# Four edits to a four-layer hybrid decoder trunk: selection in steps, table copies moved, memory loads held, one rotary product for two groups

## The chip, the cores and the metric

The kernel runs on one core of a Trainium2 chip. The metric is the time of one execution on the device in microseconds; lower is better. One profiled execution gives the trace. Engines: TensorE (PE, with its weight loads as PEld), VectorE (DVE), ScalarE (ACT), GpSimd (POOL) and SyncE (SP). SP issues most DMAs from its own queue, POOL the rest.

## The reference, cut to what matters

A sequence of 256 tokens of width 2048 passes four layers. Each layer normalises, makes one wide input projection, runs one self mixer and a cross-attention over a memory of 256 tokens, gates both with SiLU, projects out and adds to the residual. The mixers are, in order, latent attention (0), sparse attention with key selection (1), window attention with sinks (2) and latent attention again (0).

```python
mem_n = _rmsnorm(mem, mem_norm)
for i in range(DEPTH):
    h = _rmsnorm(x, norm_in[i])
    kind, j = i % N_MIXERS, i // N_MIXERS
    # self_out, mq, gate from the mixer of this kind
    mem_out = _memory_attention(mq, mem_n @ w_mem_kv[i])
    y = jnp.concatenate([self_out, mem_out], axis=-1) * jax.nn.silu(gate)
    x = x + y @ w_out[i]
return _rmsnorm(x, final_norm)
```

In latent attention, queries come from a compressed vector: `q = (_rmsnorm(c_q) @ w_uq)`, 16 heads of 128 plain and 64 rotary features; the rotary part is rotated, and so is one rotary key shared by all heads. In sparse attention a small indexer scores every key for every query (16 index heads, ReLU, weighted sum), the 64 best keys of each query are kept, and a position bias from a table of 32 buckets x 32 heads is added to the logits. Window attention adds the same bias inside a window of 128.

## The kernel before, in words

All products are float32, done as three products of float32r parts: a high part (`copy_act` on ACT, L60) and a low part (`tensor_sub` on DVE, L64). Every weight block is split that way after its load, into `wh` and `wl` (three buffers each, `parts_of`). `stage` (L190) loads one block of weights on the SP queue into `wr`, five buffers of up to 512 KB. `rows_by` (L212) gives outputs with tokens on partitions: for each 128 rows of weights, six matmuls, 2 token halves x 3 parts, as wide as the columns asked for (up to 512). `columns_by` (L232) gives outputs with features on partitions: for each 128 rows, two wide matmuls (512) and two narrow ones (256). Both accumulate in PSUM tiles with the tag "acc", four buffers.

The kernel is written as one straight program. A scheduler with a time simulation reorders the instructions of each engine when the program is built, in general in the order they were written in, as operands and buffers become ready. What goes through `tc.keep_in_program_order` stays behind whatever was written before it on its engine. Tiles with one tag share a few buffers: "pq" has five, "aux" three ("PQ, AUX, WR" at L28).

**Memory stage** (`memory`, L305). For each layer and each half of the heads: a value product (`acc_mv`), two key products (`acc_mk`), whose results POOL stores to DRAM (`mv`, `mkT`). In the first step two bias tables are computed (`bias_table`, L116); one for sparse attention, one for window attention. `table_copies` (L130) then writes each table, a quarter at a time, to DRAM once for each of 128 partitions, so that a later load (`bm`, L775) can read it shifted by one element per partition. In the memory stage one such copy follows each step, two follow the second (L384).

**Layers** (L821). `mixer.first()` makes keys and values. For latent attention it makes the compressed key/value rows and the rotary key with two 288-column products (`acc_kva`, `acc_kvb`), and then the compressed queries (`acc_cq`). Then six parts follow in the order memory 0, self 0 to 3, memory 1. Each part has a projection, an attention, and an output product of its quarter (`w_out`, L827: four column blocks `c`), written one part later. The memory part (`memory_project`, L476) loads its stored keys and values on POOL (`mkr`, tag "pq"; `mvr`, tag "aux"), makes its queries (`acc_mq`) and its gate (`acc_g`, two halves of one `columns_by` each).

A latent self part (`Latent.project`, L605) handles a group of four heads: the rotary query product (`acc_qr`, 4 heads x 64 = 256 columns, 12 row blocks), its rotation (`rope`, L528), split and transposes to `qrT`; then plain queries `acc_qn`, keys `acc_kn`, values `acc_va`, and the gate.

A sparse or window layer (`Grouped`, L664) has `first`, which in the sparse layer calls `select` (L719). `select` makes the index queries (`acc_iq`) and then, for two halves of the queries, 16 score steps (two matmuls `isp`, a ReLU on ACT, a weighted sum on DVE) and 8 steps that each find and strike out the 8 largest scores (`max`, `match_replace`). Behind it `first` clears and fills the spaced values `vz` with POOL, ACT and DVE.

Of the kernel before, what the change touches and what calls it, by code (L numbers as in the profile page):

```python
# [15 lines left out]
P = 128  # L16
S = 256
# [9 lines left out]
N_TAB = 384  # L27
PQ, AUX, WR = 5, 3, 5  # L28


@with_exitstack
def kernel(ctx: ExitStack, tc: tile.TileContext, a: dict, out: bass.AP,
# [97 lines left out]
    def table_copies(v, g):  # L130
        src = bass.AP(tensor=flat[v].tensor, offset=flat[v].offset + g * 8 * N_TAB,
                      ap=[[0, P], [1, 8 * N_TAB]])
        tc.keep_in_program_order(nc.gpsimd.dma_start(tabs[v][g].rearrange("p h n -> p (h n)"), src))


    def rsqrt_mean(dst, ssq, n):
# [53 lines left out]
    def stage(w, k0, m, cols):  # L190
# [13 lines left out]
        return wr, n  # L204

    def parts_of(wr, c0, n):
        wh = wp.tile([P, 512], F32R, name="wh", tag="wh", bufs=3)
        wl = wp.tile([P, 512], F32R, name="wl", tag="wl", bufs=3)
        split(wh[:, :n], wl[:, :n], wr[:, c0:c0 + n])
        return wh, wl  # L210

    def rows_by(xt, kts, w, k0, cols, name, prepare=None):  # L212


        acc = [ps.tile([P, 512], F32, name=f"acc_{name}{t}", tag="acc", bufs=4) for t in range(2)]
        for s in range(0, kts, ST):
            m = min(ST, kts - s)
            wr, n = stage(w, k0 + s, m, cols)
            if prepare is not None and s % 4 == 0:
                prepare(s // 4)  # L220
            for k in range(m):
                wh, wl = parts_of(wr, k * n, n)
                q = xt[(s + k) // 4]
                for t in range(2):
                    xh, xl = (q[:, v, (s + k) % 4, t * P:(t + 1) * P] for v in range(2))
                    first, last = s + k == 0, s + k == kts - 1
                    nc.tensor.matmul(acc[t][:, :n], xh, wh[:, :n], start=first, stop=False)  # L227
                    nc.tensor.matmul(acc[t][:, :n], xh, wl[:, :n], start=False, stop=False)  # L228
                    nc.tensor.matmul(acc[t][:, :n], xl, wh[:, :n], start=False, stop=last)  # L229
        return acc  # L230

    def columns_by(xt, kts, w, k0, cols, name):  # L232

        acc = [ps.tile([P, 2, S], F32, name=f"acc_{name}{j}", tag="acc", bufs=4) for j in range(2)]
        for s in range(0, kts, 2 * ST):
            m = min(2 * ST, kts - s)
            wr, n = stage(w, k0 + s, m, cols)
            for k2 in range(0, m, 2):
                wh, wl = parts_of(wr, k2 * S, 2 * S)
                for k in range(2):  # L240
                    kt = s + k2 + k
                    q = xt[kt // 4]

                    for j in range(2):
                        o = k * S + j * P
                        nc.tensor.matmul(acc[j], wh[:, o:o + P], q[:, :, kt % 4, :],  # L246
                                         start=kt == 0, stop=False)
                    for j in range(2):
                        o = k * S + j * P
                        nc.tensor.matmul(acc[j][:, 0, :], wl[:, o:o + P], q[:, 0, kt % 4, :],  # L250
                                         start=False, stop=kt == kts - 1)
        return acc
# [52 lines left out]
    def memory():  # L305
# [49 lines left out]

        copies = [(v, g) for v in range(2) for g in range(4)]
        for i in range(depth):
            w = a["w_mem_kv"][i]
            for p_ in range(2):
# [22 lines left out]
                if step == 6:  # L382
                    nm.finish()
                for c in copies[:2 if step == 1 else 1]:  # L384
                    table_copies(*c)
                copies = copies[2 if step == 1 else 1:]

# [87 lines left out]

    def memory_project(nm, i, w, mq0, g0, part):  # L476
        kT, qT = [], []
        v = [act.tile([P, 2, 512], F32R, name="mvr", tag="aux", bufs=AUX) for z in range(2)]
        for z in range(2):
            nc.gpsimd.dma_start(v[z], mv[i][part][:, z])  # L480
        for h in range(2):
            k = act.tile([P, 2, 2, S], F32R, name="mkr", tag="pq", bufs=PQ)
            nc.gpsimd.dma_start(k, mkT[i][2 * part + h])
            kT.append(k)
# [54 lines left out]
    class Latent:  # L539
# [6 lines left out]
        def first(self):  # L546
# [55 lines left out]
            for z, sg in zip(self.scale, (1.0, -1.0)):  # L602
                nc.vector.tensor_scalar(z, qr, sg * (A_NOPE + A_ROPE) ** -0.5, None, op0=OP.mult)

        def project(self, g):  # L605

            j = self.j
            wq, wkv = a["w_uq"][j], a["w_ukv"][j]
            qn, kn = [], []
            qr = act.tile([P, 4, S], F32R, name="qrT", tag="aux", bufs=AUX)  # L610
            v = act.tile([P, 2, 512], F32, name="va", tag="aux", bufs=AUX)
            acc = rows_by(self.cT[:3], 12, wq, 0, (g * 768, 4, 192, A_NOPE, A_ROPE), "qr")
            for t in range(2):
                rr = wk.tile([P, 4, A_ROPE], F32, name="qrr", tag="z", bufs=3)
                rope(rr, acc[t][:, :S].rearrange("p (h d) -> p h d", h=4), t, 4)
                rs = wk.tile([P, 4, 2, A_ROPE], F32R, name="qrs", tag="qrs", bufs=1)
                split(rs[:, :, 0, :], rs[:, :, 1, :], rr)
                transposed(lambda i0, i1: qr[:, i0:i1, t * P:(t + 1) * P],
                           [rs[:, h].rearrange("p a b -> p (a b)") for h in range(4)])
            for half in range(2):  # L620
# [10 lines left out]
            for t in range(2):  # L631
                copy_act(v[:, t, :], acc[t])
            return qn, qr, kn, v, gate(self.nm, self.w, self.g0 + g * 512)

# [29 lines left out]
    class Grouped:  # L664
# [7 lines left out]
        def first(self):  # L672
# [10 lines left out]
            if self.sparse:  # L683
                self.select()

# [33 lines left out]
        def select(self):  # L719
# [5 lines left out]
            for n in (8, 4, 4):  # L725
# [10 lines left out]
                h0 += n  # L736
            nc.vector.tensor_scalar(iw, iw, 0.25, None, op0=OP.mult)
            for b in range(2):
                n = (b + 1) * P
                sco = [wk.tile([P, S], F32, name=f"sco{z}", tag=f"sco{z}", bufs=1) for z in range(2)]  # L740
                cur = 0
                for h in range(16):
# [9 lines left out]
                    else:  # L752
                        nc.vector.scalar_tensor_tensor(sco[1 - cur][:, :n], rl[:, :n], c,
                                                       sco[cur][:, :n], op0=OP.mult, op1=OP.add)
                        cur = 1 - cur
                nc.vector.tensor_add(sco[1 - cur][:, :n], sco[cur][:, :n], caus[:, S - n:])
                cur = 1 - cur
                for it in range(8):
                    m8 = small("m8", 8)
                    nc.vector.max(m8, sco[cur][:, :n])  # L760
                    nc.vector.match_replace(sco[1 - cur][:, :n], m8, sco[cur][:, :n], TAKEN)
                    cur = 1 - cur
                nc.vector.tensor_scalar(self.sel[:, b, :n], sco[cur][:, :n], -2e38, NEG,
                                        op0=OP.is_gt, op1=OP.mult)

        def project(self, g):
# [11 lines left out]

        def attend(self, g, q, bm, gT):
            y = act.tile([P, 2, 4, S], F32R, name="y", tag="y", bufs=2)  # L780
            for h in range(8):
# [35 lines left out]

    nm = Norm(0)
    memory()

    for i in range(depth):  # L821
# [5 lines left out]
        def w_out(part, y, last):  # L827
            for c in range(4):
                acc = rows_by([y], 4, a["w_out"][i], part * 4, (c * 512, 512), "wo")
                for t in range(2):  # L830
                    xs = x[t][:, c * 512:(c + 1) * 512]
                    nc.vector.tensor_add(xs, xs, acc[t])  # L832
                if last and nxt is not None:
                    nxt.chunk(c)
# [10 lines left out]
        for n_, part in enumerate(order):  # L845
            if part >= 4:
                y = memory_attend(*memory_project(nm, i, mixer.w, mixer.mq0, mixer.g0, part - 4))
            else:
# [90 lines left out]
```

## Time and profile before

| | |
|---|---|
| time, median of 3 runs | 2635.22 us (2634.94 to 2639.01) |
| time of the profiled execution | 2636.8 us |
| its span in the profile | 2634.7 us |
| TensorE busy | 2601.2 us, 99% of the span |
| VectorE, ScalarE busy | 1884.1 us (72%), 1628.8 us (62%) |
| GpSimd busy | 57.3 us (2%) |
| moved by DMA | 511.70 MB, 194 GB/s in the mean |
| DMA in the first six of 40 slices | 256 to 305 GB/s, busy share 0.8 to over 0.9 |

TensorE's busy time is that of pipelined instructions, so 99% says that it hardly waits, and not that each matmul runs at its best; what one costs is read from the distance between starts. The memory stage fills the first 370 us or so; the four layers follow.

### The profile page before, as it was taken

How to read it: one execution, taken by the hardware profiler on the slowest of the kernel's cores; microseconds unless marked ns; L12 is line 12 of the kernel's file. 1: busy time of each engine (PE TensorE's matmuls, PEld its weight loads, DVE VectorE, ACT ScalarE, POOL GpSimd, SP SyncE). 2: the span in 40 equal slices, each digit the busy share in tenths (PEclk: the TensorE clock that was granted, in tenths of full speed). 3: DMA queues.
4: the chain of work that ended last, by engine and by line, in shares of the span. 5: the costliest groups of instructions: out<-in, count | busy, mean ns of one | idle time of the engine just before them, and what ended most of it. 6: DMA issues, size and time to landing. Idle time of an engine off the chain costs nothing.

```text
span 2634.7 us, 42943 instructions
## 1 busy us (share of the span) xinstructions
PE 2601.2 (99%) x14556; PEld 2254.7 (86%) x14556; DVE 1884.1 (72%) x4171; ACT 1628.8 (62%) x3476; POOL 57.3 (2%) x101
## 2 busy tenths in 40 slices
PE   8999999999999999999999999999999999999998
PEld 7888888888888889888888888888888888888886
DVE  6566656677767685877777776777778767776767
ACT  6455556556656566666666666676666655665655
POOL 1000000000000000000000000000000000000000
PEclk9999999999999999999999999999999999999999
DMA  9889886666557665555555555555555666655764
GB/s 305 279 287 300 281 256 198 166 185 168 169 160 224 192 192 172 167 183 170 173 163 191 188 190 177 173 172 178 189 168 162 205 165 186 165 170 156 226 183 135
DMA packets 456924, 511.70 MB, mean 194 GB/s; under 512 B 69584, under 2 KB 352480, under 8 KB 455552
## 3 DMA queue, kind: packets, MB, share of 16 engines
q1 hardware_dynamic: 443328, 451.75, 56.5%
q0 software_dynamic: 13088, 56.16, 6.6%
q8 instruction: 114, 1.87, 0.3%
q14 instruction: 106, 0.87, 0.1%
q10 hardware_dynamic: 288, 1.05, 0.1%
HBM read 489.91 MB, written 31.56 MB: 198 GB/s over the span
## 4 chain that ended last, share of the span: by engine, by line
PE 97%; DMA 1%; DVE 1%; ACT 0%; issue 0%; SPq 0%; ACTq 0%
PE acc_g L246 14%; PE acc_g L250 7%; PE acc_wo L227 7%; PE acc_wo L228 7%; PE acc_wo L229 7%; PE acc_mq L246 5%; PE acc_mk L246 5%; PE acc_qn L246 3%; PE acc_cq L246 3%; PE acc_mq L250 2%; PE acc_mk L250 2%; PE acc_q L227 2%; PE acc_q L228 2%; PE acc_q L229 2%; PE acc_mv L227 2%; PE acc_mv L228 2%
## 5 line engine op out<-in xcount | busy, mean ns | idle before, releaser
L64 DVE TENSOR_TENSOR wl<-wr,wh 128x512 fp32r<-128x512 f32 (+2 forms) x1776 | 1173.8, 664 | 645.1 <-ACT wh L60 614.2
L60 ACT ACTIVATE wh<-wr 128x512 fp32r<-128x512 f32 (+2 forms) x1776 | 1079.0, 609 | 837.3 <-PE acc_g L246 183.7
L246 PE MATMUL acc_g<-xT,wh 128*128 128x512 f32 x1536 | 489.0, 397 | 0.6 <-DVE z L257 0.6
L250 PEld LDWEIGHTS acc_g<-xT,wl 128*128 128x128 f32 x1536 | 285.2, 188 | 60.7
L250 PE MATMUL acc_g<-xT,wl 128*128 128x256 f32 x1536 | 311.0, 280 | 0.0
L228 PE MATMUL acc_wo<-wl,y 128*128 128x512 f32 x768 | 302.6, 394 | 0.6 <-DVE wl L64 0.5
L229 PE MATMUL acc_wo<-wh,y 128*128 128x512 f32 x768 | 299.1, 390 | 0.0
L246 PEld LDWEIGHTS acc_g<-xT,wh 128*128 128x128 f32 x1536 | 238.1, 189 | 4.8 <-issue 1.1
L227 PE MATMUL acc_wo<-wh,y 128*128 128x512 f32 x768 | 240.4, 393 | 0.7 <-ACT wh L60 0.6
L228 PEld LDWEIGHTS acc_wo<-wl,y 128*128 128x128 f32 x768 | 144.3, 188 | 30.0 <-DVE wl L64 1.4
L229 PEld LDWEIGHTS acc_wo<-wh,y 128*128 128x128 f32 x768 | 144.2, 188 | 28.4
L227 PEld LDWEIGHTS acc_wo<-wh,y 128*128 128x128 f32 x768 | 141.3, 188 | 27.8 <-ACT wh L60 1.0
L246 PE MATMUL acc_mk<-mT,wh 128*128 128x512 f32 x512 | 161.9, 398 | 2.4 <-ACT wh L60 2.4
L246 PE MATMUL acc_mq<-xT,wh 128*128 128x512 f32 x512 | 161.7, 397 | 0.0
L832 DVE TENSOR_TENSOR x<-x,acc_wo 128x512 f32<-128x512 f32 x192 | 125.7, 683 | 7.1 <-PE acc_wo L229 6.8
L246 PE MATMUL acc_qn<-cT,wh 128*128 128x512 f32 x384 | 123.2, 399 | 0.0
L246 PE MATMUL acc_cq<-xT,wh 128*128 128x512 f32 x384 | 120.8, 396 | 0.0
L250 PEld LDWEIGHTS acc_mk<-mT,wl 128*128 128x128 f32 x512 | 96.7, 189 | 23.4 <-DVE wl L64 0.8
L250 PEld LDWEIGHTS acc_mq<-xT,wl 128*128 128x128 f32 x512 | 93.7, 188 | 20.0
L250 PE MATMUL acc_mq<-xT,wl 128*128 128x256 f32 x512 | 102.5, 281 | 0.0
L228 PE MATMUL acc_q<-wl,xT 128*128 128x512 f32 x256 | 102.4, 400 | 0.0
L250 PE MATMUL acc_mk<-mT,wl 128*128 128x256 f32 x512 | 101.7, 280 | 0.0
(280 smaller groups left out, 4438.0 us busy)
## 6 DMA issues: line engine op xcount, KB each, us to landing
wr<-in_w_out_dram SPq DMA_DIRECT2D x192, 512.0 KB, 3.7
wr<-in_w_in_a_dram SPq DMA_DIRECT2D x176, 512.0 KB, 4.1
wr<-in_w_mem_kv_dram SPq DMA_DIRECT2D x128, 512.0 KB, 5.6
wr<-in_w_in_b_dram SPq DMA_DIRECT2D x112, 512.0 KB, 3.5
wr<-in_w_in_c_dram SPq DMA_DIRECT2D x104, 512.0 KB, 3.5
wr<-in_w_uq_dram SPq DMA_DIRECT2D x288, 128.0 KB, 2.6
tab<-flat POOLq DMA_DIRECT2D x8, 1536.0 KB, 11.1
wr<-in_w_in_a_dram SPq DMA_DIRECT2D x32, 288.0 KB, 3.0
```

The costliest lines, as they stand in the source:

```text
L60: nc.scalar.activation(o, i, AF.Copy, scale=scale)
L64: nc.vector.tensor_sub(lo, src, f32(hi))
L227: nc.tensor.matmul(acc[t][:, :n], xh, wh[:, :n], start=first, stop=False)
L228: nc.tensor.matmul(acc[t][:, :n], xh, wl[:, :n], start=False, stop=False)
L229: nc.tensor.matmul(acc[t][:, :n], xl, wh[:, :n], start=False, stop=last)
L246: nc.tensor.matmul(acc[j], wh[:, o:o + P], q[:, :, kt % 4, :], start=kt == 0, stop=False)
L250: nc.tensor.matmul(acc[j][:, 0, :], wl[:, o:o + P], q[:, 0, kt % 4, :], start=False, stop=kt == kts - 1)
L832: nc.vector.tensor_add(xs, xs, acc[t])
```

## The change

Four edits go together.

1. `select` returns a generator. Each of its 32 score steps and 16 top-8 steps ends in a `yield`. `stage`'s callers call `other_work` after each weight block is requested, which takes two steps. The spaced values move to the end of the generator. What is left is drained at the start of the first self attention.
2. The eight `table_copies` leave the memory stage. Each now follows the first column block of an output product: six in layer 0, two in layer 1. A one-column POOL copy of the new residual (`not_before`) is pinned ahead of each.
3. The loads of the first memory part of each layer are pinned on POOL behind a `not_before` on the layer's own keys (`mixer.k`, or the rotary key `mixer.kr`).
4. The rotary query product is made once for two groups (8 heads x 64 = 512 columns), behind the values and ahead of the gate of the even group. The "aux" tag has five buffers instead of three, and the scratch for POOL's DMA descriptors is given as 8192 bytes.

```diff
-PQ, AUX, WR = 5, 3, 5
+PQ, AUX, WR = 5, 5, 5
...
+    def not_before(col):
+        tc.keep_in_program_order(nc.gpsimd.tensor_copy(small("tick", 1), col))
...
+    steps = []
+    def other_work():
+        for _ in range(2):
+            if steps and next(steps[0], None) is None:
+                steps.pop()
...
             wr, n = stage(w, k0 + s, m, cols)
+            other_work()
...
-        copies = [(v, g) for v in range(2) for g in range(4)]
...
-                for c in copies[:2 if step == 1 else 1]:
-                    table_copies(*c)
-                copies = copies[2 if step == 1 else 1:]
...
-    def memory_project(nm, i, w, mq0, g0, part):
+    def memory_project(nm, i, w, mq0, g0, part, behind):
         kT, qT = [], []
+        if part == 0:
+            not_before(behind)
         v = [act.tile([P, 2, 512], F32R, name="mvr", tag="aux", bufs=AUX) for z in range(2)]
+        pin = tc.keep_in_program_order if part == 0 else lambda inst: inst
         for z in range(2):
-            nc.gpsimd.dma_start(v[z], mv[i][part][:, z])
+            pin(nc.gpsimd.dma_start(v[z], mv[i][part][:, z]))
         for h in range(2):
             k = act.tile([P, 2, 2, S], F32R, name="mkr", tag="pq", bufs=PQ)
-            nc.gpsimd.dma_start(k, mkT[i][2 * part + h])
+            pin(nc.gpsimd.dma_start(k, mkT[i][2 * part + h]))
...
+        def rotary(self, g):
+            self.qr = [act.tile([P, 4, S], F32R, name="qrT", tag="aux", bufs=AUX) for z in range(2)]
+            acc = rows_by(self.cT[:3], 12, a["w_uq"][self.j], 0, (g * 768, 8, 192, A_NOPE, A_ROPE), "qr")
+            for t in range(2):
+                for z in range(2):
+                    rr = wk.tile([P, 4, A_ROPE], F32, name="qrr", tag="z", bufs=3)
+                    rope(rr, acc[t][:, z * S:(z + 1) * S].rearrange("p (h d) -> p h d", h=4), t, 4)
+                    rs = wk.tile([P, 4, 2, A_ROPE], F32R, name="qrs", tag="qrs", bufs=1)
+                    split(rs[:, :, 0, :], rs[:, :, 1, :], rr)
+                    transposed(lambda i0, i1: self.qr[z][:, i0:i1, t * P:(t + 1) * P],
+                               [rs[:, h].rearrange("p a b -> p (a b)") for h in range(4)])
...
-            acc = rows_by(self.cT[:3], 12, wq, 0, (g * 768, 4, 192, A_NOPE, A_ROPE), "qr")
...
-            return qn, qr, kn, v, gate(self.nm, self.w, self.g0 + g * 512)
+            if g % 2 == 0:
+                self.rotary(g)
+            return qn, self.qr[g % 2], kn, v, gate(self.nm, self.w, self.g0 + g * 512)
...
             if self.sparse:
-                self.select()
+                steps.append(self.select())
+            else:
+                self.spaced_values()
...
+            return self.selection(iqT, ikd, iw)
+        def selection(self, iqT, ikd, iw):
...
+                    yield True
...
+            self.spaced_values()
...
         def attend(self, g, q, bm, gT):
+            while steps:
+                other_work()
...
+                if c == 0 and copies:
+                    not_before(xs[:, :1])
+                    table_copies(*copies.pop(0))
...
-    nc = _bacc.Bacc("TRN2", target_bir_lowering=False, num_devices=1)
+    nc = _bacc.Bacc("TRN2", target_bir_lowering=False, num_devices=1,
+                     dynamic_dma_scratch_size=8192)
```

More of the change, by code (lines that the diff above doesn't have):

```diff
@@ L609, in project @@
             qn, kn = [], []
-            qr = act.tile([P, 4, S], F32R, name="qrT", tag="aux", bufs=AUX)
             v = act.tile([P, 2, 512], F32, name="va", tag="aux", bufs=AUX)
-            acc = rows_by(self.cT[:3], 12, wq, 0, (g * 768, 4, 192, A_NOPE, A_ROPE), "qr")
[L613 to L619, printed above, removed]
             for half in range(2):
@@ L683, in first, with spaced_values @@
             if self.sparse:
-                self.select()
+                steps.append(self.select())
+            else:
+                self.spaced_values()
+        def spaced_values(self):
             self.vz = [act.tile([P, 2, 9 * 64], F32R, name="vz", tag=f"big{1 + z}") for z in range(2)]
@@ L779, in attend @@
         def attend(self, g, q, bm, gT):
+            while steps:
+                other_work()
             y = act.tile([P, 2, 4, S], F32R, name="y", tag="y", bufs=2)
@@ L819 @@
     memory()
+    copies = [(v, g) for v in range(2) for g in range(4)]
     for i in range(depth):
@@ L846 @@
             if part >= 4:
-                y = memory_attend(*memory_project(nm, i, mixer.w, mixer.mq0, mixer.g0, part - 4))
+                y = memory_attend(*memory_project(nm, i, mixer.w, mixer.mq0, mixer.g0, part - 4,
+                                                  f32(mixer.k[:, 0] if kind else mixer.kr)[:, 0, :1]))
             else:
```

1 line of the change is left out of this document (added).

## The prediction

> **What bounds the kernel now.** I read the page first, then what TensorE waited for, then the chain that ended last, then the timeline of TensorE and of the POOL queue at the places those two name.
>
> ```profile
> span 2634.7 us, 42943 instructions
> PE 2601.2 (99%) x14556; PEld 2254.7 (86%) x14556; DVE 1884.1 (72%) x4171; ACT 1628.8 (62%) x3476; POOL 57.3 (2%) x101
> ```
>
> TensorE is busy 99% of the span: 2634.7 - 2601.2 = 33.5 us are idle, and of these the start (before the first weights) and the tail take most. A change can only win by giving TensorE less to stream or by closing one of its few gaps. Its waits, summed by line:
>
> ```profile
> PE acc_mv L227 <- ACT wh L60: 10.0, 2, 8.7
> PE acc_kvb L227 <- ACT wh L60: 3.1, 1, 3.1
> PE acc_mk L246 <- ACT wh L60: 2.4, 1, 2.4
> ```
>
> The 8.7 us is the start. That leaves three gaps, and the chain (start, length) shows a DMA behind each; its first two rows are there for the spacing of undisturbed matmuls, 18 of them from one row to the next:
>
> ```profile
> 103.54 0.45 PE acc_mv L227 x2
> 107.62 0.45 PE acc_mv L227 x2
> ...
> 110.40 15.19 DMA wr<-in_w_mem_kv_dram
> 284.38 6.88 DMA ft<-in_l_x_dram
> 381.13 10.21 DMA wr<-in_w_in_a_dram
> ```
>
> So 4.08 / 18 = 0.227 us for a matmul of 512 columns. TensorE's timeline gives the size of the gaps (start, duration):
>
> ```profile
> 123.55 0.39 PE L229 MATMUL acc_mv<-wh,mT 128*128 128x512 f32 x1
> 126.38 0.73 PE L246 MATMUL acc_mk<-mT,wh 128*128 128x512 f32 x2 [2.44 <-ACT wh L60]
> 131.06 0.62 PE L246 MATMUL acc_mk<-mT,wh 128*128 128x512 f32 x2
> ...
> 291.92 0.39 PE L229 MATMUL acc_mv<-wh,mT 128*128 128x512 f32 x1
> 293.57 0.73 PE L227 MATMUL acc_mv<-wh,mT 128*128 128x512 f32 x2 [1.26 <-ACT wh L60]
> ...
> 387.87 0.42 PE L227 MATMUL acc_kvb<-wh,xT 128*128 128x288 f32 x2
> 388.53 0.29 PE L229 MATMUL acc_kvb<-wh,xT 128*128 128x288 f32 x1
> 391.92 0.53 PE L227 MATMUL acc_kvb<-wh,xT 128*128 128x288 f32 x2 [3.11 <-ACT wh L60]
> 396.96 0.43 PE L227 MATMUL acc_kvb<-wh,xT 128*128 128x288 f32 x2
> ```
>
> And the POOL queue shows what was sent just before the first and the last:
>
> ```profile
> 107.69 1.06 POOL L133 DMA_DIRECT2D tab<-flat  x2
> 379.88 1.08 POOL L480 DMA_DIRECT2D mvr<-mv  x2
> 380.93 0.56 POOL L483 DMA_DIRECT2D mkr<-mkT  x1
> ```
>
> The last two views I look at are stretches: one around the first gap, one where the key selection runs (columns: PE, PEld, DVE, ACT, POOL busy, then granted clock, DMA share, GB/s).
>
> ```profile
> 120.00:140.00 20.00, 17.56 (x85) 14.50 (x84) 9.26 (x14) 8.38 (x15) 1.09 (x2) 0.91 1.00 315
> 1080.00:1100.00 20.00, 20.00 (x124) 17.83 (x123) 18.77 (x55) 12.40 (x30) 1.06 (x1) 1.00 0.51 157
> ```
>
> **The change part by part.** *Table copies.* Eight copies of 1.5 MB leave the memory stage; six go behind the first output product of each part of layer 0, two into layer 1. In the memory stage two went out together at 107.69, and the weight block requested at 110.40 took 15.19 us. DMA share was 1.00. TensorE stood from 123.55 + 0.23 (a matmul's spacing) to 126.38, so 2.6 us. It then ran slowly: four groups of two wide and two narrow matmuls, from 126.38 to 131.06, took 4.7 us, where 0.227 for a wide and about half of it for a narrow one make 4 x 0.68 = 2.7. That is the granted clock of 0.91 in that row, and 1.9 us more (I round down for the narrow ones). Sum 4.5 us. I expect all of it back: nothing else was sent at that moment. The gap at 291.92 (1.65 - 0.23 = 1.4 us) hangs on input rows in the SP queue, which a fuller DMA delays; the copies are one cause among several, so I take half, 0.7 us.
>
> In their new place the copies meet the output weights. Rows of the DMA view (KB each, median us to landing):
>
> ```profile
> wr<-in_w_out_dram SPq DMA_DIRECT2D x192, 512.0 KB, 3.7
> tab<-flat POOLq DMA_DIRECT2D x8, 1536.0 KB, 11.1
> ```
>
> A weight block of 512 KB feeds 12 wide matmuls, 12 x 0.227 = 2.7 us; with five buffers a block is requested four blocks, 10.9 us, ahead. One 1.5 MB copy is half of the pair that made 15.19, and the pair overran by 2.6, so a landing up to about 12.6 us is hidden. Above the 3.7 us of quiet a single copy adds about half of 15.19 - 3.7, 5.7 us: 9.4 us, hidden. So I price the eight at nothing; the other end is half the pair's 4.5 us each, 8 x 2.25 = 18 us lost. Single copies in the memory stage made no gap of their own, which is the nearest row. Each copy has a one-column POOL copy ahead that waits for the residual addition. Behind it in the POOL queue stand only loads for later parts, tens of us early; POOL is 2% busy.
>
> *First memory keys held back.* Loads for a layer's first part now wait on POOL until the layer's own keys exist. In layer 0 they left at 379.88 to 381 (1.5 MB) into the narrow 288-column product, where matmuls are 0.132 apart (five of them from 387.87 to 388.53), so that a block lasts only 12 x 0.132 = 1.6 us and the lead is 6.3 us: the block of 381.13 took 10.21 and TensorE stood from 388.53 + 0.13 to 391.92, 3.3 us, then ran the next 24 matmuls to 396.96 in 5.04 us instead of 24 x 0.132 = 3.2. Sum 5.1 us. After the change they leave behind that product, among blocks with the long lead: gone. They are then needed by the memory attention, four weight products later (some 45 us against landings of at most 10): hidden. What is new: the pinned loads, four of 512 KB, and with five "aux" buffers instead of three the values of the second memory part as well, can leave in one burst of 3 MB in layers 1 and 2. That is the size of the pair of copies. From 3.7 + 11.5 = 15.2 (its pair) down to no delay; so 0 to 4.5 us at each, 0 to 9 us. I take 1 us, since there DMA share is 0.51 (the row at 1080) and not 1.00.
>
> *One rotary product for two groups.* Eight products of 12 x 6 matmuls, 256 wide, become four, 512 wide. Spacing now, from a clean stretch of the timeline:
>
> ```profile
> 519.56 0.40 PE L227 MATMUL acc_qr<-wh,cT 128*128 128x256 f32 x2
> 525.31 0.40 PE L227 MATMUL acc_qr<-wh,cT 128*128 128x256 f32 x2
> ```
>
> 48 matmuls in 5.75 us is 119.8 ns; a wide one takes 226.7 (above). So 576 x 119.8 = 69.0 us become 288 x 226.7 = 65.3: 3.7 us won, all on TensorE and so on the path. The weight splits on ACT and DVE halve in count; neither is the bound. The Trainium skill, page "TensorE: Matmul & The Clock Gate", section "Back-to-back issue gap", gives the gap as N/2.4 plus 2.5 ns, which speaks against this step: 109.2 and 215.8 ns, so merging would win only 288 x 2.5 ns = 0.7 us. The trace's own spacing is higher at both widths and I go by it; the rule makes a rival below.
>
> The rotation itself, 4 heads and 128 rows at a time, stays 16 times, but in bursts of four behind one another (one buffer "qrs"). Each is five operations on DVE, two of half the width and three like these:
>
> ```profile
> L535 DVE TENSOR_TENSOR qrr<-acc_qr,cos x16: 412/416/423, 529.5 to 2448.2; 128x256 f32<-128x256 f32 x16
> L64 DVE TENSOR_TENSOR qrs<-qrr,qrs x16: 419/424/427, 533.4 to 2453.8; 128x256 fp32r<-128x256 f32 x16
> ...
> 652.00:663.20 11.20, 11.20 (x66) 9.75 (x65) 5.71 (x9) 5.87 (x11) 0.00 (x0) 1.00 0.71 212
> ```
>
> With 0.42 for the three and, estimated from the width, 0.28 for the two halves: 1.8 us together, 7.3 us a burst. They fall into the first half of the gate product, whose stretch (last row) has DVE at 5.7 of 11.2 us: 13.0 us of work for 11.2. If DVE took the burst first, weight splits would be 1.8 us late at four places, 7 us; spread over the whole gate product there is room. I take nothing, since the rotations of today sit between splits with no gap on TensorE.
>
> *Selection step by step.* The 32 score steps and 16 top-8 steps are handed out two to a weight block instead of written in one piece. The row at 1080, in the midst of today's selection, shows TensorE busy 20.00 of 20 us although DVE is at 18.77: there is no gap to close, so it wins nothing. It can cost if it ends late:
>
> ```profile
> 1128.61 0.28 DVE L763 TENSOR_SCALAR vs<-sco 128x256 f32<-128x256 f32 x1
> 1175.53 0.28 PE L811 MATMUL o<-pT,vz 128*128 128x256 f32 x1
> ```
>
> Its end is at 1128.6 now, and the first product that needs the spaced values is at 1175.5, 47 us later. Written two to a block it lasts 24 blocks of 2.8 us, 67 us from the start of the memory queries: 16 blocks of memory queries and gate, then the eight of the first self queries. The first self group's gate product, 22 us, still lies between its last step and that first product, so it is hidden; if that cover went, a lateness of some 5 us would show, once.
>
> *Smaller scratch for POOL's descriptors.* No row shows it. If loads had to wait for one another, POOL idles and they are early: nothing; the other end is a late burst as above, within its 9 us.
>
> Sum: -4.5 - 0.7 - 5.1 - 3.7 + 1 = -13.0 us. The profiled execution took 2636.8 us (span 2634.7 plus 2.1), 1.6 over the median of the runs, 2635.2. So 2623.8 by the profile and 2622.2 by the median: I say 2622.5.
>
> **The rivals.** *A: gaps only move.* The copies and the bursts open new gaps in layers 0 to 2. For it: a 3 MB burst did so at 107.69, and each half-clock spell adds 1.9 us. Against: outside the memory stage and the narrow product the trace has no gap behind a DMA. At four such gaps, 4 x 2.25 = 9 us come back: 2631.5, no change that can be told.
>
> *B: merging wins next to nothing.* If the wide matmuls of this product came at nearly twice the narrow spacing, 239 ns and not 226.7, next to nothing is won: 2622.5 + 3.7 = 2626. Against: the value product, the same kind of matmul, is at 226.7 (rows above). By the rule of the page named above it would be 2625.5; the trace does not agree with it.
>
> *C, slower: the even groups' scores come late.* The rotary product moves from the head of a group's work to just ahead of the gate product. Rows of the transposes (the third is a summary, durations then first and last start):
>
> ```profile
> 621.44 0.28 PE L229 MATMUL acc_qr<-wh,cT 128*128 128x256 f32 x1
> 628.61 0.46 PE L395 MATMUL tr<-identr,qrs 128*128 128x128 f32 x4
> 632.71 0.46 PE L395 MATMUL tr<-identr,qrs 128*128 128x128 f32 x4
> L395 PE MATMUL tr<-identr,qrs x8: 223/238/252, 544.7 to 550.1; 128*128 128x128 f32 x8
> 652.03 0.62 PE L246 MATMUL acc_g<-xT,wh 128*128 128x512 f32 x2
> 674.32 0.63 PE L227 MATMUL acc_wo<-wh,y 128*128 128x512 f32 x2
> ```
>
> In the second group the first four transposes come 7.2 us after the product and the next 4.1 later. A burst of four would end at 7.2 + 3 x 4.1 = 19.5 us, inside the gate product's 22.3 (652.03 to 674.32). At the first group's pace (15.9 us, then about 5) it would end at 31, 9 us past it. TensorE then stands unless the output product of the part before fills in, which has 22 us of its own. From 22.3 us on it decides: up to 9 us at four places, 36 us, 2658.
>
> *D: the copies were not the cause.* Were the first gap due to the weight stream alone, 4.5 us stay: 2627. Against: it is the only place with two copies, and the only wait of that size among the key products.
>
> **How the numbers follow.** Forecast 0.56, B 0.07, D 0.06: all faster. A 0.18: within 0.2%, which is 5.3 us (2630 to 2640.5) and about what a measurement of this kernel can tell. C 0.13: slower, though small cases of it (under 10 us) fall into "same"; I leave it whole. Faster 0.69, same 0.18, slower 0.13. The forecast's own range is 2615 (the half taken at 291.92 is whole, other small waits of the memory stage go too, the burst costs nothing, some stalls inside the rotary products go) to 2629 (rotation burst 7 us). For 8 in 10 I add A: 2612 to 2640, leaving out C and a little below.
>
> **What would show it.** Right: no table copy before the first output product; no gap over 1 us on TensorE at the second key product of the memory stage nor in the second narrow product, and a granted clock of 1.00 through both; the rotary matmuls 288 in number, 512 wide, spaced about 0.227; a TensorE busy sum smaller by 3 to 5 us. Wrong: weight waits in layers 0 to 2 behind table or memory loads on POOL (A); spacing of the rotary matmuls at twice the old or more (B); TensorE waiting for scores of an even group or for late splits in the gate product (C); a gap near 124 us that stays (D); waits for the selection in layer 1, which I count at nothing.

## The result and the profile after

The changed kernel takes 2625.28 us (median of 5, 2624.62 to 2626.74) against 2635.22: a ratio of 0.9960, with a 95% interval of 0.9946 to 0.9973. It is 9.9 us faster; the forecast was 2622.5, faster. The profiled execution took 2624.62 us, with a span of 2622.4, 12.3 us less than the span before. The profiled execution of before (2636.8) was 1.6 us above the median of its runs and that of the changed kernel 0.7 below its own, so the medians give the smaller difference.

The page of the changed kernel, its engines:

```profile
span 2622.4 us, 42100 instructions
PE 2593.6 (99%) x14268; PEld 2236.0 (85%) x14268; DVE 1877.0 (72%) x4123; ACT 1625.1 (62%) x3428; POOL 62.0 (2%) x113
```

TensorE has 14268 - 14556 = -288 matmuls and 7.6 us less busy time. What it waited for, the first line of the view (total, times, longest):

```profile
PE acc_mv L240 <- ACT wh L60: 10.3, 5, 8.3
```

The waits at the key products and at `acc_kvb` are gone. What stays is the start (8.3) and four short waits of value products in the memory stage, 2.0 us together. Stretches (PE, PEld, DVE, ACT, POOL busy, granted clock as a share of TensorE's full clock, DMA share, GB/s): around the old gap at 124, through the narrow product, through the first rotation burst, and through the burst of loads in layer 1:

```profile
120.00:140.00 20.00, 20.00 (x111) 16.95 (x110) 11.69 (x21) 11.81 (x23) 1.07 (x2) 1.00 0.77 245
373.00:396.00 23.00, 23.00 (x176) 23.00 (x176) 14.39 (x33) 14.44 (x34) 0.53 (x1) 1.00 0.78 225
560.00:600.00 40.00, 40.00 (x222) 34.45 (x222) 31.08 (x72) 24.90 (x50) 1.07 (x2) 1.00 0.63 194
997.00:1003.00 6.00, 6.00 (x35) 4.91 (x34) 2.87 (x6) 4.44 (x10) 3.20 (x6) 1.00 0.87 243
```

In each of them TensorE is busy throughout at a granted clock of 1.00; the first stretch holds 111 matmul records where before had 85. TensorE's timeline shows the wide rotary product and the transposes behind it:

```profile
543.73 0.62 PE L240 MATMUL acc_qr<-wh,cT 128*128 128x512 f32 x2
...
560.05 0.62 PE L260 MATMUL acc_g<-xT,wh 128*128 128x512 f32 x2
566.09 0.45 PE L405 MATMUL tr<-identr,qrs 128*128 128x128 f32 x4
...
579.27 0.46 PE L405 MATMUL tr<-identr,qrs 128*128 128x128 f32 x4
579.87 0.28 PE L669 MATMUL sp<-kr,qrT 128*128 128x256 f32 x1
```

72 matmuls in 560.05 - 543.73 = 16.32 us: 226.7 ns each. POOL's queue shows where the held loads and the first copy went, and where the clears of the spaced values stand now:

```profile
402.88 0.20 POOL L137 COPY tick<-kr 128x1 f32<-128x1 f32 x1 [26.69 <-ACT kr L60]
403.11 1.07 POOL L493 DMA_DIRECT2D mvr<-mv  x2
404.16 1.08 POOL L496 DMA_DIRECT2D mkr<-mkT  x2
...
592.49 0.55 POOL L133 DMA_DIRECT2D tab<-flat  x1
...
997.25 1.08 POOL L493 DMA_DIRECT2D mvr<-mv  x2 [0.32 <-PE acc_iq L242]
998.32 0.55 POOL L496 DMA_DIRECT2D mkr<-mkT  x1
998.84 1.08 POOL L493 DMA_DIRECT2D mvr<-mv  x2
999.88 0.57 POOL L496 DMA_DIRECT2D mkr<-mkT  x1
1090.94 1.06 POOL L712 MEMSET vz<- 128x1152 f32 x1 [90.48 <-PE isp L772]
```

Where the 12.3 us of span went, by the starts of stages on TensorE (first matmul of a product to first matmul of the next; worked out from both timelines, as are all stage lengths below):

| stage | before | after | difference | predicted |
|---|---|---|---|---|
| start | 8.73 | 8.30 | -0.4 | 0 |
| memory stage | 365.71 | 362.44 | -3.3 | -5.2 (copies) |
| `acc_kva` and `acc_kvb` of layer 0 | 30.42 | 25.28 | -5.1 | -5.1 (held loads) |
| rest of layer 0 | 572.91 | 570.97 | -1.9 | -1.85 (rotary) |
| layer 1 | 553.13 | 553.00 | -0.1 | +0.5 (burst), 0 (selection) |
| layer 2 | 490.45 | 490.34 | -0.1 | +0.5 (burst) |
| layer 3 and tail | 613.40 | 612.09 | -1.3 | -1.85 (rotary) |

Layer 3 alone, up to the last matmul, is 1.9 shorter; the tail behind it was 0.6 longer.

### The profile page after: what moved, and what is told of

The parts are those of the page before. It is cut to its first block, busy times and chain, and to the rows that moved or that the text cites. A ratio compares the mean times of both kernels' runs of the same rounds, so it can differ in the third digit from the quotient of the medians.

```text
span 2622.4 us, 42100 instructions
## 1 busy us (share of the span) xinstructions
PE 2593.6 (99%) x14268; PEld 2236.0 (85%) x14268; DVE 1877.0 (72%) x4123; ACT 1625.1 (62%) x3428; POOL 62.0 (2%) x113
## 4 chain that ended last, share of the span: by engine, by line
PE 97%; DMA 1%; ACT 1%; DVE 1%; issue 0%; SPq 0%; ACTq 0%
PE acc_g L260 14%; PE acc_g L264 7%; PE acc_wo L241 7%; PE acc_wo L240 7%; PE acc_wo L242 7%; PE acc_mq L260 5%; PE acc_mk L260 4%; PE acc_cq L260 3%; PE acc_qn L260 3%; PE acc_mq L264 2%; PE acc_q L240 2%; PE acc_q L241 2%; PE acc_q L242 2%; PE acc_mk L264 2%; PE acc_mv L240 2%; PE acc_mv L241 2%
```

## The experiments

Each session ran the kernel before again, at medians of 2635.1 to 2637.1 us; the ratios are against these.

**Each edit alone.** The theory is that of the prediction: rotary, copies and held loads win separately, the selection nothing. The rivals are B and C for the rotary product, D for the copies, and that the edits only work together. The first kernel has edit 4 only, with its five "aux" buffers and the smaller scratch.

```diff
-PQ, AUX, WR = 5, 3, 5
+PQ, AUX, WR = 5, 5, 5
...
+        def rotary(self, g):
...
+            acc = rows_by(self.cT[:3], 12, a["w_uq"][self.j], 0, (g * 768, 8, 192, A_NOPE, A_ROPE), "qr")
...
+            if g % 2 == 0:
+                self.rotary(g)
```

> The one rotary product for two groups alone (with five aux buffers and the small descriptor scratch, which it needs for room); everything else as before. My theory: TensorE streams 3.7 us less, 1.9 in layer 0 and 1.9 in layer 3, no new wait: about 2631.5, and the three gaps at 124, 292 and 389 us stay. Rival B (wide matmuls cost twice the narrow ones): 2635, no change. Rival C (late scores or late splits): over 2637, with TensorE waits in the gate products.

Measured: 2632.88 us, ratio 0.9993 (0.9984 to 1.0001). By itself the time can't be told from no change, but the stages can: layer 0 is 1.91 us shorter behind `acc_cq`, layer 3 1.88, all others up to the last matmul, but for the memory stage and the narrow product, stand within 0.1. That is 3.8 us for 288 merged pairs, 13 ns each. Its wait at the narrow product stayed. TensorE's waits show it:

```profile
PE acc_kvb L227 <- ACT wh L60: 3.0, 1, 3.0
```

The stretch around it (columns as above), in this kernel:

```profile
385.00:400.00 15.00, 12.04 (x90) 11.62 (x89) 6.70 (x15) 7.21 (x17) 0.00 (x0) 1.00 0.85 264
```

And the stretch in the kernel before:

```profile
388.00:400.00 12.00, 8.89 (x55) 8.47 (x54) 4.04 (x9) 4.33 (x10) 0.00 (x0) 0.86 0.73 227
```

Before's 3.1 us was followed by half clock (0.50 from 393.31 to 396.72 us, 0.86 in the mean of this stretch); this 3.0 us was not, and the narrow products took 28.73 us instead of 30.42. So a gap of nearly one size has two prices.

Edit 2 alone moves the copies behind the output products:

```diff
-                for c in copies[:2 if step == 1 else 1]:
-                    table_copies(*c)
...
+                if c == 0 and copies:
+                    not_before(xs[:, :1])
+                    table_copies(*copies.pop(0))
```

> The table copies moved behind the output products, alone. My theory: the memory stage gets shorter by 3 to 4.5 us (the gap at 124 us and the half clock after it go), layer 0 is not longer: about 2631.5. Rival A (the gap only moves): layer 0 longer by 2 us or more, total within 2 us of before. Rival D (the copies were not the cause): the gap at 124 us stays, 2635.

Measured: 2633.38 us, ratio 0.9995 (0.9985 to 1.0004), which can't be told from no change either. The memory stage is 362.31, 3.4 us less than the profile before, and layer 0 is not longer (504.66 against 504.68 from its memory queries on). Its waits:

```profile
PE acc_mv L232 <- ACT wh L60: 10.1, 5, 8.3
PE acc_kvb L232 <- ACT wh L60: 3.2, 1, 3.2
```

The wait at the key products is gone, four of the value products are there, as in the changed kernel. So D falls as to the gap's cause; its size is another matter (below). The half of the gap at 291.92 that I gave to the copies has no support: such waits stay without any copy in the stage. With the wait of 3.2 us at the narrow product came 6.8 us of half clock here (from 386.97 to 393.79), and the two products took 31.31 us.

Edit 3 alone holds the first memory loads:

```diff
+        if part == 0:
+            not_before(behind)
...
+        pin = tc.keep_in_program_order if part == 0 else lambda inst: inst
...
+            pin(nc.gpsimd.dma_start(v[z], mv[i][part][:, z]))
...
+            pin(nc.gpsimd.dma_start(k, mkT[i][2 * part + h]))
```

> The first memory part's loads held behind the layer's own keys, alone. My theory: the wait of 3.3 us in the second narrow product goes and so does the half clock after it, 5.1 us in all, nothing is lost elsewhere: about 2630. Rival A: the wait moves into the compressed query product or to the first products of layers 1 and 2 and half or more comes back: 2632.5 to 2635. A second rival: the wait was the last table copy's doing and not the loads': no change.

Measured: 2646.05 us, ratio 1.0041 (1.0028 to 1.0053): slower by 10.9 us. The two narrow products are 25.28, 5.1 us shorter, as expected. But in layer 1 the stretch from the memory queries to the first self queries grew from 54.89 to 69.67 us, 14.8 more. Its waits of TensorE show two that no kernel above has:

```profile
PE isp L753 <- ACT rl L756: 5.6, 1, 5.6
PE acc_g L251 <- DVE mqT L271: 3.5, 1, 3.5
```

POOL's queue in layer 1 of this kernel:

```profile
1088.39 1.06 POOL L697 MEMSET vz<- 128x1152 f32 x1 [9.47 <-PE isp L753]
1089.40 0.18 POOL L138 COPY tick<-kd 128x1 f32<-128x1 f32 x1
1089.52 1.05 POOL L488 DMA_DIRECT2D mvr<-mv  x2
1090.56 1.08 POOL L491 DMA_DIRECT2D mkr<-mkT  x2
```

And TensorE's timeline at the same time:

```profile
1075.49 2.25 PE L753 MATMUL isp<-ikd,iqT 128*128 128x256 f32 x16
1083.30 4.98 PE L753 MATMUL isp<-ikd,iqT 128*128 128x256 f32 x16 [5.55 <-ACT rl L756]
1091.75 0.79 PE L251 MATMUL acc_g<-xT,wh 128*128 128x512 f32 x1 [3.47 <-DVE mqT L271]
```

The pinned loads stand behind the clears of the spaced values, and the second clear waits for the last score matmul, whose operand `iqT` has the same buffers ("big1", "big2"). So the memory keys leave at 1090 instead of shortly after the layer's keys. TensorE has nothing but the selection's last 32 score matmuls from 1075.5 on, at the pace of ReLU and weighted sum; then it waits for the memory queries `mqT`. Two gaps, 5.55 + 3.47 = 9.0 us; and behind the first the same 16 matmuls took 4.98 instead of 2.25 us, at half clock (0.50 from 1081.37 to 1095.02). Why `mqT` itself came only at 1088.5, behind the ReLUs, I read from the code: it and the held keys take turns in the "pq" buffers, and these are handed out in the order written. The trace shows only that `mqT` stands behind ten ReLUs in ScalarE's order, and it was made before the held keys even left (1090.56), so this last link is argued and not shown.

Edit 1 alone hands out the selection:

```diff
-                self.select()
+                steps.append(self.select())
+            else:
+                self.spaced_values()
...
+            while steps:
+                other_work()
...
```

> The key selection in steps, alone. My theory: TensorE had no gap there, so nothing is won and nothing lost: 2635 within 1 us, layer 1 as long as before within 0.5 us. Rival (a late selection): layer 1 longer by up to 5 us with a wait at the first self attention. Rival (the burst had slowed TensorE without a gap): layer 1 shorter by 2 us or more.

Measured: 2636.47 us, ratio 1.0007 (0.9999 to 1.0016). In layer 1 the stretch up to the first self queries is 1.96 us shorter, the next up to the first product with spaced values 3.25 longer, the rest 1.50 shorter: -0.2 in all. It moves matmuls from one stretch to the next and wins nothing, as predicted.

So the sum of the edits done alone is -2.24 - 1.74 + 10.93 + 1.35 = +8.3 us by their medians, and together they give -9.9. The difference sits in layer 1: edit 3 costs 15 us there without edit 1. Two kernels ask which part of edit 1 takes that cost away: the steps, or the place of the clears. The first is the changed kernel with the selection in one piece, its clears ahead of the pinned loads:

```diff
-                steps.append(self.select())
+                for _ in self.select():
+                    pass
```

> The changed kernel with the key selection written in one piece again, its clears of the spaced values ahead of the pinned memory loads. My new theory: the pinned loads then stand behind clears that wait for the last score matmul, the query buffers stand behind the loads, and TensorE runs out of other work: layer 1 longer by 13 to 15 us, as it was with the loads held back alone, 2637 to 2640. Rival (that loss came with three aux buffers only): layer 1 as in the changed kernel, 2622 to 2626.

Measured: 2642.08 us, ratio 1.0024 (1.0015 to 1.0033). This kernel has five "aux" buffers, so the three of the kernel with edit 3 alone were not the cause of its loss. The second has the same and writes the spaced values at the start of the first self attention, so in one piece but behind the loads:

```diff
-            self.spaced_values()
...
-            while steps:
-                other_work()
+            if self.sparse and g == 0:
+                self.spaced_values()
```

> The selection in one piece as in the run beside it, but with the clears and the spaced values written at the start of the first self attention, behind the pinned loads. My new theory: only the order of the clears and the pinned loads matters, not the steps: as fast as the changed kernel within 1 us, 2622 to 2626. Rival (the selection in one piece is what holds TensorE): layer 1 longer by 5 to 15 us.

Measured: 2625.46 us, ratio 0.9964 (0.9952 to 0.9976), the changed kernel's time; from the memory queries to the end of layer 1 it takes 0.1 us less than in the kernel before. POOL's queue of the kernel in one piece, clears ahead:

```profile
1085.75 1.06 POOL L713 MEMSET vz<- 128x1152 f32 x1 [9.47 <-PE isp L773]
...
1086.88 1.09 POOL L493 DMA_DIRECT2D mvr<-mv  x2
```

POOL's queue of the kernel with the clears late:

```profile
997.85 1.09 POOL L493 DMA_DIRECT2D mvr<-mv  x2 [0.32 <-PE acc_iq L242]
...
1094.88 1.07 POOL L713 MEMSET vz<- 128x1152 f32 x1 [16.90 <-ACT rl L776]
```

The loads leave 89 us earlier (997.85 against 1086.88), and 16.6 us come back. So the steps are worth nothing here; that the clears (moved together with the filling of the spaced values) come behind the pinned loads is worth about 15 to 17 us once the loads are pinned.

**What the copies cost, and what hides them.** Before, with one copy a step and never a pair:

```diff
-                for c in copies[:2 if step == 1 else 1]:
+                for c in copies[:1]:
...
-                copies = copies[2 if step == 1 else 1:]
+                copies = copies[1:]
```

> The kernel before with one table copy behind each of the eight memory steps, no pair; all copies stay in the memory stage. If the pair is what makes the gap at 124 us (as the prediction had it), that gap goes and the memory stage is 2 to 4.5 us shorter, as with the copies moved out: 2631 to 2633. If the stage is simply full, copies and all, a single copy leaves a gap there too, of 1 us or more: 2634 to 2636.

Measured: 2636.73 us, ratio 1.0001 (0.9992 to 1.0010). No gap is left at 124, and the memory stage is 363.12. But the eighth copy now leaves at 378.04, among the weights of the narrow products, and these took 32.68 us, 2.3 longer than before. POOL's queue has it:

```profile
378.04 0.53 POOL L133 DMA_DIRECT2D tab<-flat  x1
```

TensorE's waits show what it does, 4.7 us where the kernel before has 3.1:

```profile
PE acc_kvb L227 <- ACT wh L60: 4.7, 1, 4.7
```

The pair did make the gap at 124. That the single copy lengthened the gap among the short blocks is likely and not shown: the kernel with edit 1 alone, with no copy there, has 4.3 us at this place and 31.45 us of narrow products. In the other direction, the changed kernel with two copies behind each of the first four output products:

```diff
+PAIR = 2
...
-                    table_copies(*copies.pop(0))
+                    for _ in range(min(PAIR, len(copies))):
+                        table_copies(*copies.pop(0))
```

> The changed kernel with two table copies instead of one behind each of the first four output products of layer 0. By the prediction's reckoning a pair makes a weight block land after 3.7 + 11.5 = 15 us, 2.6 us later than can be hidden: a gap of 1 to 3 us and perhaps a half-clock spell at each of four places, 8 to 18 us longer. Rival: layer 0 asks for less of the DMA than the memory stage did, so even a pair is hidden: no change within 1 us.

Measured: 2625.63 us, ratio 0.9964 (0.9950 to 0.9977). Layer 0 is 0.2 us longer than with singles, and no gap came. The DMA view gives a copy's landing (KB, median us); first the changed kernel, with the weight blocks requested beside its first copy (593 to 598 us):

```profile
tab<-flat POOLq DMA_DIRECT2D x8, 1536.0 KB, 9.1
wr<-in_w_uq_dram SPq DMA_DIRECT2D x8, 128.0 KB, 7.9
```

Then the kernel with pairs (blocks from 592 to 596 us):

```profile
tab<-flat POOLq DMA_DIRECT2D x8, 1536.0 KB, 11.7
wr<-in_w_uq_dram SPq DMA_DIRECT2D x6, 128.0 KB, 13.0
```

And the stretch behind its first pair (columns as above):

```profile
590.00:610.00 20.00, 20.00 (x102) 16.93 (x101) 14.21 (x33) 12.12 (x27) 1.59 (x3) 1.00 0.90 272
```

TensorE does not notice even the pair, but the weights do: they land 5 us later than beside a single copy, and ScalarE's first split of them waits until 606.37. They are hidden because of what they are. The blocks requested behind the copies are small ones of the next query product, not the output weights that the prediction took: the first is requested at 592.62, and its product starts at 607.67, a lead of 15.1 us where the prediction had 10.9. The DMA share is lower as well, 0.90 where the memory stage had 1.00; how much of the difference is due to that, no run here separates.

**The waits that stayed in the memory stage.** The chain of the changed kernel at one of the four (start, length):

```profile
191.09 6.15 DMA ft<-in_l_x_dram
197.26 0.70 ACT xT L60 x2
...
198.97 0.53 ACT wh L60
199.55 0.73 PE acc_mv L240 x2
```

ScalarE's timeline at that place:

```profile
195.02 0.63 ACT L60 ACTIVATE wh<-wr 128x512 fp32r<-128x512 f32 x1
197.26 1.71 ACT L60 ACTIVATE xT<-ft,gvec 128x256 fp32r<-128x256 f32 x4 [1.61 <-DMA ft<-in_l_x_dram]
198.88 1.66 ACT L60 ACTIVATE wh<-wr 128x512 fp32r<-128x512 f32 x3
```

ScalarE weights a quarter of the decoder's input rows (`ft`) between weight splits. The rows are requested at 191.09, their weighting stands in ScalarE's order at 197.26, and the splits `wh` behind it are late by as much as the rows are. Other profiles of this stage have three or four such waits, the longest 2.0 us. The theory: request the rows a step earlier and the wait goes. The rival: something else holds the splits.

```diff
...
-                    nm.chunk(step - 2)
+                    nm.chunk(step - 2, xft.pop(0))
+                if 1 <= step < 5:
+                    xft.append(features(a["l_x"], step - 1))
```

> The changed kernel with the feature-major input rows of the next layer requested one memory step (some 45 us) earlier; nothing left out. My theory: what is left in the memory stage are four waits of ScalarE on these rows, requested only 6 us before they are used, each holding the weight splits behind them: 0.5 to 0.8 us of TensorE plus 0.16 after it. All four go, 3.3 us won: span 2619 against 2622.4. Rival (the splits wait on the weight blocks as well): half of it or less, 2621 or more.

Measured: 2624.51 us, ratio 0.9957 (0.9945 to 0.9970). Two waits at value products are still there, 1.5 us together where the changed kernel had 2.0. The chain of this kernel shows why:

```profile
191.36 6.04 DMA ft<-in_l_x_dram
197.43 0.70 ACT xT L60 x2
```

The scheduler drew the weighting forward with the load: it still stands right where the rows land. The remedy fell, not the theory; so the weighting is pinned in ScalarE's order as well:

```diff
-            copy_act(dst[:, 0, k, :], src[:, k, :], scale=g)
+            pin(nc.scalar.activation(dst[:, 0, k, :], src[:, k, :], AF.Copy, scale=g))
...
```

> The changed kernel with the input rows requested one memory step early, and ScalarE's weighting of them pinned behind that step's other work, so that it cannot be drawn ahead to the moment they land (as it was without the pin, where the four waits stayed). My theory: the weighting finds its rows some 40 us old; the four waits of 0.5 to 1.2 us at the value products go: memory stage 2.5 to 3.3 us shorter, span 2619 to 2620. Rival (the weight blocks are late there as well): the waits stay at half or more, 2621 or more.

Measured: 2621.85 us, ratio 0.9947 (0.9933 to 0.9960), the lowest of all, its interval overlapping that of the changed kernel. TensorE's waits: the four are gone, and two others came:

```profile
PE acc_mv L240 <- ACT wh L60: 8.2, 1, 8.2
PE acc_mk L260 <- ACT wh L60: 1.8, 2, 1.0
```

Their chain leads to another set of rows (`x`, 7.17 us from 262.96) and ScalarE's squares of them. So these were requested a step earlier too, and the squares pinned:

```diff
-        nc.scalar.activation(junk[:, :src.shape[-1]], src, AF.Square, accum_out=col)
+        pin(nc.scalar.activation(junk[:, :src.shape[-1]], src, AF.Square, accum_out=col))
...
+                    first_rows(step - 1)
...
```

> The changed kernel with both forms of the input rows requested one memory step early, and both the weighting and the squares of them pinned on ScalarE behind that step's other work. With the weighting alone pinned, the waits had moved to the squares (1.0 and 1.2 us). My theory: now nothing on ScalarE meets a fresh load, the memory stage has no wait over 0.5 us on TensorE and is 2 to 3 us shorter than the changed kernel's: span 2619 to 2620.5. Rival (a wait always finds the next load): a wait of about 1 us remains, on the weight blocks, span 2621 to 2622.

Measured: 2625.07 us, ratio 0.9954 (0.9940 to 0.9968): a miss, with four waits of 0.8 us. At the first of the old places no row is late any more, but ScalarE's timeline shows its own work instead:

```profile
149.35 1.70 ACT L185 ACTIVATE xT<-ft,gvec 128x256 fp32r<-128x256 f32 x4
150.95 0.62 ACT L191 ACTIVATE junk<-x 128x512 f32<-128x512 f32 x1
...
152.18 1.66 ACT L60 ACTIVATE wh<-wr 128x512 fp32r<-128x512 f32 x3
```

Pinned in one piece, weighting and squares take 152.18 - 149.35 = 2.8 us ahead of the splits, and TensorE waits 0.8 us for them at 152.84. With the work spread by the scheduler, it waited for the rows; pinned, for the work. For scale, the changed kernel itself ran beside that one, without an edit:

> The changed kernel itself once more, beside the run above on the same chip: span 2622 to 2624, four waits of 0.5 to 0.8 us in the memory stage, so that the difference of the two is that of the memory stage alone.

Measured: 2625.82 us, ratio 0.9957 (0.9944 to 0.9970), 11.3 us under the kernel before in the same session, where the first result was 9.9. The expectation of its span and of four waits missed: the span is 2624.7, and three such waits stand there, 2.6 us together and the longest 1.4. Its memory stage took 364.33 us in this profile, 362.44 in the first, and 361.5 to 364.9 over the six profiles that share this stage. That scatter is as large as what these three kernels were to win. I don't call any of them better than the changed kernel; whether the 3.4 us of the pinned weighting are real stays open.

## Why the prediction was right, and where it was not

The sum was -13.0 us and the result -9.9 by the medians, -12.3 by the two profiles. Its terms:

**Held loads, -5.1.** Right in place and size. 25.28 us stands in every kernel that holds them, against 28.73, 30.42 and 31.45 in three profiles where copies and loads are as before, and 31.31 with the copies alone moved. What it is worth is not one number, though: the half clock behind the gap comes in some executions only.

**Rotary product, -3.7.** Right: 3.8, at the 226.7 ns that I took. B falls. The Trainium skill, page "TensorE: Matmul & The Clock Gate", section "Back-to-back issue gap", gives N/2.4 + 2.5 ns for a matmul by itself, by which this step would win an estimated 0.7 us; the trace does not agree with it (226.7 ns instead of 215.8 at 512 columns).

C falls, by the step that I weighed: the burst's last transposes start 579.27 - 560.05 = 19.2 us behind the product, where 19.5 was worked out at the second group's pace, and the scores follow at once, inside the gate product. The rotations of 7.3 us on DVE made no split late: TensorE is busy 40.00 of 40 us there, and no wait over 0.7 us stands in any layer of the changed kernel.

**Copies, -4.5 and -0.7.** The mechanism was right and the size off. The gap at 124 belongs to the pair (gone in every kernel without it), but I read its price from one profile, in which half clock followed the gap: the waits at the key products sum to 1.2, 2.8 and 2.4 us in the three other profiles that have the pair, and only some go on at half clock. Over these four the memory stage takes 363.9 to 366.3 us, mean 365.0; over the six profiles with the copies moved and nothing else changed in the stage, 361.5 to 364.9, mean 363.1. So the term measures 1.9 us where 5.2 stood, and the ranges overlap. The 0.7 for the gap at 291.92 is not borne out: the wait at this place is 0 to 1.4 us in the six profiles without copies and 0.3 to 1.3 us in the four with them, and its chain leads to the rows and to ScalarE's order.

With the mean for the copies the sum is -5.1 - 3.8 - 1.9 = -10.8, close to the -9.9 of the medians and the -11.3 of the later session.

**The copies' new place, 0.** Right in size, wrong in its reason. The prediction weighed the copies against 512 KB blocks of output weights with a lead of 10.9 us; at the copies looked at, the blocks behind them are those of the next query product, with a lead of 15.1 us. Its landing of 9.4 us beside a single copy is not far off (7.9 at the median), but it would have a pair overrun, and the pairs did not.

**The burst, +1.** It left as described, 997.25 to 1000.45, at a DMA share of 0.87, and cost nothing. A falls with it.

**The selection, 0.** Right as a sum and wrong as a reading. I priced edit 3 by its loads' landing and edit 1 by DVE's free time, each alone. I did write that a pinned load waits in POOL's queue, but looked only at what stands behind it, not at what stands ahead: two clears that wait for the last score matmul. Of the four edits this pair is coupled, at 15 to 17 us, more than the whole gain. The forecast held because the change moves the clears behind the loads, a line I had put down as "the spaced values move" and priced at nothing. That was luck.

## What to carry to other kernels

Pinning a load in a queue makes it wait for everything written before it there: list that work and what each item waits for, before pricing the load. Price edits in pairs where they meet in a queue or a buffer ring, not only one by one. And a stage whose length scatters by 2 us from execution to execution can't give a term of 5 us from one profile.

## What the runs showed of the hardware

A gap that the waits view gives as 2.4 us (before, ahead of 126.38) was followed by a granted clock of 0.50 from 127.07 to 130.48 us; one of 3.0 us (rotary product alone, ahead of 389.74) was not, with 1.00 from 380 to 410. The spells at 0.50 last 3.4 us (before, twice), 6.8 (copies alone, from 386.97) and 13.65 (held loads alone, from 1081.37), close to whole multiples of 3.4. The Trainium skill, page "TensorE: Matmul & The Clock Gate", section "What's actually happening", has the throttle come after at least one idle window of about 3.4 us, and says that the window runs free. The lengths of the spells and the varying price agree with windows of that kind; a plain bound of 3.4 us on the idle time does not, since 2.4 were enough.

Of two copies of 1.5 MB between DRAM buffers sent together (the kernel with pairs), the first landed 8.8 to 10.3 us after its issue and the second 13.1 to 13.7; the 11.7 of the DMA view lies between them. Both were done some 14 us after the first issue, where one alone took 9.1 at the median. In the memory stage of the kernel before, with a DMA share of 1.00, the two of the pair took 11.7 and 16.3 us.
